# Seven block products for eight in the output projection of six token-tile pairs

## The chip, the cores and the metric

The kernel runs on one core of one Trainium2 chip. The metric is device microseconds for one execution of the whole program. Within the core, TensorE (PE; its weight loads are PEld) multiplies into PSUM; VectorE (DVE), ScalarE (ACT) and GpSimd (POOL) work on tiles in SBUF; SyncE (SP) and ACT issue the DMAs. Each engine runs its own list of instructions strictly in order and waits at semaphores for the others.

## The reference, cut to what matters

Two groups of 1024 tokens (`g` = 0 and 1) pass through one encoder layer with shared weights. All of it is float32.

```python
h    = layer_norm(x, in_ln_g, in_ln_b)
proj = h @ w_in                        # q, k, v, gates, conv inputs, memory queries
o_da = rms_norm(softmax(q1 k1) v - lam * softmax(q2 k2) v) * silu(g_da)   # 4 heads
o_cv = b * conv3(c * h_) * silu(g_cv)
o_mx = softmax(q_m k_m) v_m * silu(g_m)                                   # 256 memory tokens
out  = concat([o_da, o_cv, o_mx]) @ w_o          # (1024 x 1024) @ (1024 x 1024)
y    = layer_norm(2 ** 0.25 * h + out, ln_g, ln_b)
```

The change concerns the last two lines. The residual `2 ** 0.25 * h` needs the mean and scale of each row of x, which are known early.

## The kernel before, in words

Every float32 product is made as three passes: each operand is split into a rounded part `hi` (float32r) and a remainder `lo`, and `hi*hi + hi*lo + lo*hi` is summed in PSUM. A pass over one 128x128 block and 512 columns is one MATMUL.

A recorder (`Flow`) sets the order. Python code runs through the PE work in order, counts it in nominal nanoseconds (`fl.pe(650)` for a step of three passes), and `after(ns, fn)` puts the instructions of other engines into their lists when that count has moved on by `ns`. These numbers only fix positions in the lists; on the chip each engine goes on as soon as its operands and buffers are there.

The body is 20 jobs: for each group, four heads and one memory job (`h` is None), each for two halves of the queries. A job has four scores (`score`: PE into two PSUM tiles `ps` of the pool `psS`, DVE takes row maxima `mx`, ACT exponentials `e`). The job before it is finished meanwhile: `turn` transposes its `e` into a `psS` tile `pt` that must have been released by ACT, ACT and DVE split `pt` into `th` and `tl`, and `av` multiplies them by v. `job_steps` puts these into slots, 20 a job; between slots `run` puts steps of the list `Fillers`, the projections, spread evenly. So `turn` comes one slot (one twentieth of the job's fillers) behind `score`.

The output projection stands at the end of the same list of fillers. `Out(g, t)` handles one tile of 128 tokens: `load` fetches the mixed heads (`mraw`) and the rows of x (`xr`); `prepare` splits `mraw` into `mixh` (ACT) and `mixl` (DVE, L160); `residual` scales x (ACT L913, DVE L914, POOL L917); `passes` makes 24 MATMULs for each half of the 1024 columns into a bank `pout` (L925), adds (L928), takes statistics (L931), and `finish` normalises with four SCALAR_TENSOR_TENSOR (L946, L949) and issues two output DMAs on ACT's queue (L954). Between L946 and L949 POOL raises the variance to -1/2 (L941, L942). `w_o` is loaded and split by `load_wo` in the last job and at the start of the projection; the first four tiles overlap the last job's `turn` and `av`. Tiles 4 to 15 stand alone.

```python
for ti, (a, b) in enumerate(((self.mh, wh), (self.mh, wl), (self.ml, wh))):
    T.matmul(self.ps, a[:, kb, :], b, start=kb == 0 and ti == 0, stop=kb == KB - 1 and ti == 2)
...
V.tensor_tensor(self.xt[:, c], self.ps, self.xt[:, c], op=ALU.add)
V.bn_stats(self.bs[:, n, :], self.xt[:, c])
```

## Time and profile before

| | us |
|---|---|
| median of three runs (1226.39 to 1227.21) | 1227.06 |
| the profiled execution, its own time | 1227.65 |
| its span, first to last instruction | 1225.8 |
| PE busy in the span (5881 MATMULs) | 1182.9 (96%) |
| DVE, ACT, POOL busy | 802.6, 425.9, 414.9 |

The profiled execution's time is 1.85 us over its span (launch and end), and 0.6 us over the median. The shares of busy time are means over stages that differ: in most of the body PE is busy almost without a break, and the other engines have room. A row of the trace gives the start, the duration, the engine, the line, the operation and output<-inputs; brackets tell how long the engine was idle before it and what released it.

### The profile page before, as it was taken

The page shows a single profiled execution, that of the slowest core. Times are in us where ns is not written, and L with a number is a line of the kernel's source. Part 1 is how long each engine was busy: PE and PEld are TensorE (multiplying, and loading weights), DVE is VectorE, ACT ScalarE, POOL GpSimd, SP SyncE. Part 2 cuts the span into 40 slices and gives each one's busy share as a digit, 9 for nine tenths or more (in the row PEclk, how much of TensorE's full clock was granted, in tenths as well). Part 3 has the DMA queues.
Part 4 walks back from the last instruction along what each step waited for, and adds up shares of the span by engine and source line. Part 5 has one row for each costly group of instructions (what it writes and reads, how often), then busy time and mean ns, then how long its engine had stood idle before and what let it go on. Part 6 is the DMA issues. An engine that isn't in the chain of part 4 may idle for free.

```text
span 1225.8 us, 15660 instructions
## 1 busy us (share of the span) xinstructions
PE 1182.9 (96%) x5881; PEld 922.5 (75%) x5881; DVE 802.6 (65%) x1156; ACT 425.9 (35%) x703; POOL 414.9 (34%) x466
## 2 busy tenths in 40 slices
PE   7899999999999999999999999999999999899997
PEld 5677777767776777778677777777777877688886
DVE  4779857665677585533667666556565456887776
ACT  4624343333332333334443323434334335212220
POOL 4754413352244340232311113023011345444443
PEclk9999999999999999999999999999999999999999
DMA  8366336433644289653312212222223359354341
GB/s 309 111 233 214 143 129 206 153 145 107 214 155 155 96 277 332 238 200 133 135 43 86 86 44 95 67 97 95 73 75 112 103 207 310 106 194 152 129 148 52
DMA packets 83644, 182.62 MB, mean 149 GB/s; under 512 B 7712, under 2 KB 26352, under 8 KB 83440
## 3 DMA queue, kind: packets, MB, share of 16 engines
q1 hardware_dynamic: 80112, 175.33, 41.0%
q10 hardware_dynamic: 3456, 6.29, 1.3%
q8 instruction: 46, 0.75, 0.2%
q14 instruction: 30, 0.25, 0.1%
HBM read 119.69 MB, written 61.91 MB: 148 GB/s over the span
## 4 chain that ended last, share of the span: by engine, by line
PE 72%; DVE 13%; ACT 4%; POOL 3%; issue 3%; DMA 3%; SPq 1%; POOLq 0%; DVEq 0%; ACTq 0%
PE pout L925 13%; PE ps L678 6%; PE pt L736 5%; DVE mx L685 3%; ACT e L686 3%; PE po L764 2%; PE pG L435 2%; PE pG L437 2%; PE pG L436 2%; PE pQ L435 2%; PE pQ L437 2%; PE pQ L436 2%; PE pV L435 2%; PE pV L436 2%; PE pV L437 2%
## 5 line engine op out<-in xcount | busy, mean ns | idle before, releaser
L686 ACT ACTIVATE e<-ps,mx 128x1024 f32<-128x1024 f32 x128 | 142.8, 1116 | 302.2 <-DVE mx L685 301.9
L685 DVE TENSOR_REDUCE mx<-ps 128x1 f32<-128x1024 f32 x128 | 150.6, 1217 | 91.4 <-PE ps L678 91.4
L925 PE MATMUL pout<-woh,mixl 128*128 128x512 f32 x256 | 100.4, 392 | 1.2 <-DVE mixl L160 1.1
L925 PE MATMUL pout<-woh,mixh 128*128 128x512 f32 x256 | 100.5, 393 | 0.0
L925 PE MATMUL pout<-wol,mixh 128*128 128x512 f32 x256 | 100.2, 391 | 0.0
L160 DVE TENSOR_TENSOR tl<-pt,th 128x1024 fp32r<-128x1024 f32 x80 | 97.2, 1216 | 3.9 <-ACT th L742 3.5
L694 DVE SCALAR_TENSOR_TENSOR e<-e,ssum,e 128x1024 f32<-128x1024 f32 x64 | 87.5, 1368 | 0.0
L742 ACT ACTIVATE th<-pt 128x1024 fp32r<-128x1024 f32 x80 | 82.1, 1026 | 12.6 <-PE pt L736 11.8
L736 PE MATMUL pt<-ident,e 128*128 128x128 f32 x512 | 67.6, 275 | 12.3 <-ACT e L686 12.3
L917 POOL TENSOR_TENSOR xr<-xr,lnrow 128x512 f32<-128x512 f32 x32 | 55.2, 1741 | 68.8 <-DVE xr L914 68.8
L736 PEld LDWEIGHTS pt<-ident,e 128*128 128x128 f32 x512 | 58.0, 141 | 26.9 <-ACT e L686 21.2
L476 POOL TENSOR_TENSOR sw<-sw,ropet 128x512 f32<-128x512 f32 x32 | 41.7, 1304 | 88.4 <-DVE sw L470 88.4
L722 POOL TENSOR_SCALAR em<-em,rm 128x256 f32<-128x256 f32 x64 | 33.4, 536 | 93.0 <-DVE rm L720 46.6
L678 PE MATMUL ps<-kh,qh 64*128 64x512 f32 x256 | 61.5, 445 | 3.2 <-DVE tl L160 2.7
L160 DVE TENSOR_TENSOR wl<-wraw,wh 128x1024 fp32r<-128x1024 f32 (+1 forms) x33 | 43.7, 1323 | 23.6 <-POOL wh L157 13.8
L925 PEld LDWEIGHTS pout<-woh,mixl 128*128 128x128 f32 x256 | 48.3, 189 | 12.4 <-DVE mixl L160 2.3
L764 PE MATMUL po<-th,vh 128*128 128x512 f32 x128 | 57.2, 447 | 0.0
L906 ACT ACTIVATE mixh<-mraw 128x1024 fp32r<-128x1024 f32 x16 | 17.0, 1060 | 115.1 <-PE pout L925 97.7
L925 PEld LDWEIGHTS pout<-wol,mixh 128*128 128x128 f32 x256 | 48.4, 189 | 10.2
L925 PEld LDWEIGHTS pout<-woh,mixh 128*128 128x128 f32 x256 | 48.3, 189 | 9.9
L678 PE MATMUL ps<-kl,qh 64*128 64x512 f32 x256 | 53.5, 391 | 1.8 <-DVE kl L479 1.8
L678 PE MATMUL ps<-kh,ql 64*128 64x512 f32 x256 | 53.2, 390 | 0.0
(284 smaller groups left out, 3069.3 us busy)
## 6 DMA issues: line engine op xcount, KB each, us to landing
wp<-w SPq DMA_DIRECT2D x80, 512.0 KB, 4.3
wraw<-in_wt SPq DMA_DIRECT2D x32, 512.0 KB, 4.5
w<-wh SPq DMA_DIRECT2D x28, 512.0 KB, 5.5
w<-wl SPq DMA_DIRECT2D x28, 512.0 KB, 3.9
mraw<-mix SPq DMA_DIRECT2D x16, 512.0 KB
xr<-in_x SPq DMA_DIRECT2D x16, 512.0 KB, 6.4
out<-xr ACTq DMA_DIRECT2D x24, 256.0 KB, 2.0
x<-in_x SPq DMA_DIRECT2D x8, 512.0 KB, 5.5
```

What stands on the lines that cost most here:

```text
L160: (eng or V).tensor_tensor(out, x, hi.bitcast(F32), op=ALU.subtract)
L435: T.matmul(ps, wh[:, k], hh, start=kb == 0, stop=False)
L436: T.matmul(ps, wh[:, k], hl, start=False, stop=False)
L437: T.matmul(ps, wl[:, k], hh, start=False, stop=kb == KB - 1)
L678: T.matmul(ps[c][:, n], q[r, qt * P:(qt + 1) * P], k[r, n], start=i == 0, stop=i == 2)
L685: V.tensor_reduce(mx[:, c:c + 1], ps[c], AX.X, ALU.max, negate=True)
L686: A.activation(e[c], ps[c], AF.Exp, bias=mx[:, c:c + 1], accum_out=sm[:, c:c + 1])
L694: V.scalar_tensor_tensor(e[0], e[1], st, e[0], op0=ALU.mult, op1=ALU.add)
L736: T.transpose(pt[:, u * HS + i * P:u * HS + (i + 1) * P], self.tiles[i][:, (b + u) * P:(b + u + 1) * P], const["ident"])
L742: A.activation(th, pt, AF.Copy)
L764: T.matmul(self.po, vh[:, k, :], th[:, c], start=k == 0, stop=False)
L925: T.matmul(self.ps, a[:, kb, :], b, start=kb == 0 and ti == 0, stop=kb == KB - 1 and ti == 2)
```

## The change

Tiles 0 to 3 of group 0 go on as before (their `Out` gets its residual ready-made). The other 12 tiles go in six `Pair`s of two neighbouring tiles. A pair is one 2x2 block product: the rows are its two tiles, the inner dimension and the columns are cut in two. It is made in Winograd's form, with 7 products of 4 k-blocks each (12 MATMULs a product, 84 a pair; before, two tiles took 96). Four sums of the left operand (S1 to S4) are made on POOL for each pair (`sums`), and split on ACT and DVE (`splits`). The four sums of blocks of `w_o` (T) are made once. The products land in four PSUM regions (`pa`, `pb`, `pcd`), and `after_product` combines them into the two residual tiles `x1`, `x2` on DVE and POOL.

What can be made early is parked in DRAM in jobs 11 to 17: `park_wo` (16 blocks of `w_o` split, and 16 sums of blocks split) and `park_residual` (16 tiles of x made into the residual, through two buffers `wraw`). `load_wo`, `load_sums`, `load_rows` and `residuals` fetch these at the end. All pairs but the last normalise their second tile by another way (`mixed`): POOL makes -mean*scale, ACT applies it to 1024 columns, DVE multiplies by `ln_g`, POOL adds `ln_b`.

`job_steps` has 28 slots instead of 20, with `turn` two slots behind `score`; scores of memory jobs come two at a time. The third pair of weight buffers (`deep`) is used up to job 9 only, since `wraw` is needed for parking.

```diff
-            out.append([lambda s=s: job.score(s)])
+            if not job.mem:
+                out.append([lambda s=s: job.score(s)])
+            else:
+                out.append([lambda i=i: job.score(i) for i in (s, s + 1)] if s % 2 == 0 else [])
...
-            out.append([lambda s=s: prev.turn(s)] if prev else [])
-            out += [[], []]
+            out += [[], [lambda s=s: prev.turn(s)] if prev else [], [], [], []]
...
+    def park_unit(n, x, dst):
+        hi = sb([P, HS], F32R, ("kmh", "kml")[n % 2], "whi")
+        hi_of(hi, x)
+        after(1500, lambda: V.tensor_tensor(x, x, hi.bitcast(F32), op=ALU.subtract))
...
+    def park_residual(i):
...
+        x = sb([P, D], F32, "wraw", "xres")
+        dma(x, X[g][t * P:(t + 1) * P, :])
+        st = stats[g]
+        after(4000, lambda: A.activation(x, x, AF.Identity, bias=st[:, 0, t:t + 1], scale=st[:, 1, t:t + 1]))
+        after(5500, lambda: V.tensor_tensor(x, x, resid["g"], op=ALU.mult))
+        for n in range(2):
+            c = slice(n * HS, n * HS + HS)
+            after(7000, lambda n=n, c=c: G.tensor_tensor(x[:, c], x[:, c], resid["b"][n], op=ALU.add))
+        after(10500, lambda: dma(r_d[g][t * P:(t + 1) * P, :], x))
...
-            raw = sb([P, HS], F32, "ev", "woraw")
-            dma(raw, wo[kb * P:(kb + 1) * P, n * HS:(n + 1) * HS])
...
+            for t, src in zip(W[kb, n], wo_d[kb, n]):
+                dma(t.bitcast(F32), src)
...
+        def close(n, c):
+            G.tensor_tensor(y[:, c], y[:, c], W["lb"][n], op=ALU.add)
+            after(2000, lambda: out(c))
...
+        nb = sb([P, 1], F32, "small", "nbo")
+        G.tensor_tensor(nb, mv[:, 0:1], ve, op=ALU.mult)
+        G.tensor_scalar(nb, nb, -1.0, 1.0, op0=ALU.mult, op1=ALU.mult)
+        after(1500, lambda: A.activation(y, y, AF.Identity, bias=nb, scale=ve))
+        for n, c in enumerate(halves):
+            after(2800 + FD * n, lambda n=n, c=c: V.tensor_tensor(y[:, c], y[:, c], W["lg"][n], op=ALU.mult))
+            after(4000 + 1700 * n, lambda n=n, c=c: close(n, c))
...
+        ORDER = (("A", 0, 0, None), ("S12", 1, 1, 1), ("A", 1, 0, None), ("S12", 0, 2, 0), ("S34", 0, 3, 2), ("S34", 1, 2, None),
+                 ("A22", 0, 3, 3))
...
+            G.tensor_tensor(s1, m2[:, lo], m2[:, hi], op=ALU.add)
+            G.tensor_tensor(s2, s1, m1[:, lo], op=ALU.subtract)
+
+            def rest():
+                G.tensor_tensor(s3, m1[:, lo], m2[:, lo], op=ALU.subtract)
+                G.tensor_tensor(s4, m1[:, hi], s2, op=ALU.subtract)
+            self.rest = after(4000, rest)
...
+            if i == 0:
+                self.s1 = sb([P, HS], F32, "ev", "s1")
+                A.activation(self.s1, f[0], AF.Copy)
+            if i == 1:
+                self.u = sb([P, HS], F32, "ev", "u")
+                V.tensor_tensor(self.u, f[1], self.s1, op=ALU.add)
+                G.tensor_tensor(x1[:, hi], x1[:, hi], self.u, op=ALU.add)
+                G.tensor_tensor(x2[:, lo], x2[:, lo], self.u, op=ALU.add)
+            if i == 2:
+                V.tensor_tensor(x1[:, lo], f[0], x1[:, lo], op=ALU.add)
+                stat_of(x1, 0, self.bs[0])
+                if nxt:
+                    nxt.sums()
+                    nxt.splits("A")
+            if i == 3:
+                self.s5 = sb([P, HS], F32, "ev", "s5")
+                A.activation(self.s5, f[2], AF.Copy)
+                G.tensor_tensor(x2[:, hi], x2[:, hi], self.s5, op=ALU.add)
+                if nxt:
+                    nxt.splits("S12")
+            if i == 4:
+                w = sb([P, HS], F32, "ev", "w7")
+                V.tensor_tensor(w, f[3], self.u, op=ALU.add)
+                V.tensor_tensor(x2[:, hi], x2[:, hi], w, op=ALU.add)
+            if i == 5:
+                V.tensor_tensor(x1[:, hi], f[2], x1[:, hi], op=ALU.add)
+                stat_of(x1, 1, self.bs[0])
+                normalise(self.g, 2 * self.p, x1, self.bs[0][0], False)
+            if i == 6:
+                V.tensor_tensor(x2[:, lo], f[3], x2[:, lo], op=ALU.add)
+                stat_of(x2, 0, self.bs[1])
+                stat_of(x2, 1, self.bs[1])
+                normalise(self.g, 2 * self.p + 1, x2, self.bs[1][0], nxt is not None)
+                if nxt:
+                    nxt.splits("S34")
+                    nxt.splits("A22")
```

The order of DVE at the boundary of two tiles before: a tile's residual multiply and split stand between the two column halves of the tile before it, and only the two last operations wait for POOL (`veo`).

```order
L914 TENSOR_TENSOR xr<-xr,lnrow_9155 128x1024
L160 TENSOR_TENSOR mixl<-mraw,mixh 128x1024
L928 TENSOR_TENSOR xr<-pout,xr 128x512
L931 BN_STATS bso<-xr 128x6
L939 BN_AGGR mvo<-bso 128x2
L946 SCALAR_TENSOR_TENSOR xr<-xr,mvo,lnrow_9221 128x512 x2
L949 SCALAR_TENSOR_TENSOR xr<-xr,veo,lnrow_9223 128x512 x2
```

The order of DVE now, from the last statistics of one pair, through the first three products of the next, into its last ones (`al`, `sh` and `a2l` are remainders of a pair's operands, made while the pair before it is multiplied; L1033 is the multiply of the mixed normalisation):

```order
L1000 BN_AGGR mvo<-bso 128x2
L161 TENSOR_TENSOR sh<-sums,sh 128x512 x2
L161 TENSOR_TENSOR a2l<-mraw,a2h 128x512
L1033 TENSOR_TENSOR xr<-xr,lg 128x512 x2
L1147 TENSOR_TENSOR u<-pb,s_10550 128x512
L1151 TENSOR_TENSOR xr<-pa,xr 128x512
L996 BN_STATS bso<-xr 128x6
L161 TENSOR_TENSOR al<-mraw,ah 128x1024
L161 TENSOR_TENSOR sh<-sums,sh 128x512 x2
L1164 TENSOR_TENSOR w_10642<-pcd,u 128x512
L1165 TENSOR_TENSOR xr<-xr,w_10642 128x512
L1167 TENSOR_TENSOR xr<-pcd,xr 128x512
```

The multiply L1033, which needs POOL's `nbo` and then ACT, has come to stand ahead of `u` and of every split that follows.

The order of POOL in one tile before:

```order
L917 TENSOR_TENSOR xr<-xr,lnrow_9157 128x512 x2
L941 TENSOR_SCALAR veo<-mvo 128x1
L942 TENSOR_TENSOR veo<-veo,mhalf 128x1
```

The order of POOL now, in the same stretch as DVE's (two more pairs of `veo` follow; the sums are those of the next pair):

```order
L1029 TENSOR_TENSOR nbo<-mvo,veo 128x1
L1030 TENSOR_SCALAR nbo<-nbo 128x1
L1021 TENSOR_TENSOR xr<-xr,lb 128x512
L1148 TENSOR_TENSOR xr<-xr,u 128x512
L1149 TENSOR_TENSOR xr<-xr,u 128x512
L1021 TENSOR_TENSOR xr<-xr,lb 128x512
L1091 TENSOR_TENSOR sums<-mraw 128x512
L1092 TENSOR_TENSOR sums<-sums,mraw 128x512
L1159 TENSOR_TENSOR xr<-xr,s_10619 128x512
L1095 TENSOR_TENSOR sums<-mraw 128x512
L1096 TENSOR_TENSOR sums<-mraw,sums 128x512
```

A pair has nine operations of 512 columns on POOL, where two tiles had four, and the sums of the next pair stand behind the finish of the pair before.

The order of PE at a `turn` before, in the first job of group 1's heads:

```order
L766 MATMUL po<-tl,vh 128x512
L435 MATMUL pQ<-hTh_1_4604,wp 128x512
L436 MATMUL pQ<-hTl_1_4605,wp 128x512
L437 MATMUL pQ<-hTh_1_4604,wp 128x512
L736 MATMUL pt<-ident,e_5452 128x128
```

The order of PE at the same place now:

```order
L777 MATMUL po<-tl,vh 128x512
L446 MATMUL pQ<-hTh_1_4608,wp 128x512
L447 MATMUL pQ<-hTl_1_4609,wp 128x512
L448 MATMUL pQ<-hTh_1_4608,wp 128x512
L446 MATMUL pQ<-hTh_1_4610,wp 128x512
L447 MATMUL pQ<-hTl_1_4611,wp 128x512
L448 MATMUL pQ<-hTh_1_4610,wp 128x512
L747 MATMUL pt<-ident,e_5456 128x128
```

One filler step of three MATMULs has moved from behind the transposes to ahead of them; so it is in nearly every head job.

## Rows read from the trace of the kernel before

**Rows 1.** Windows: from:to, us; each engine busy (count); PEclk; DMA share; GB/s.
```profile
600.00:818.00 218.00, 212.37 (x1086) 160.60 (x1086) 140.41 (x207) 84.67 (x132) 35.80 (x40) 1.00 0.23 80
818.00:932.00 114.00, 113.47 (x584) 88.45 (x582) 66.79 (x101) 40.27 (x63) 21.97 (x29) 1.00 0.25 87
...
1080.00:1218.00 138.00, 137.82 (x608) 113.64 (x606) 102.95 (x141) 24.19 (x22) 63.09 (x50) 1.00 0.38 135
...
1048.00:1054.00 6.00, 5.51 (x21) 4.50 (x22) 5.90 (x8) 1.29 (x2) 2.92 (x4) 0.72 0.51 172
```

**Rows 2.** Timeline of DVE over one tile of the output projection: start, us, what.
```profile
1141.70 0.69 DVE L928 TENSOR_TENSOR xr<-pout,xr 128x512 f32<-128x512 f32 x1 [0.83 <-PE pout L925]
1142.42 0.69 DVE L931 BATCH_NORM_STATS2 bso<-xr 128x6 f32<-128x512 f32 x1
1143.15 0.21 DVE L939 BATCH_NORM_AGGREGATE mvo<-bso 128x2 f32<-128x12 f32 x1
1143.40 1.42 DVE L946 SCALAR_TENSOR_TENSOR xr<-xr,mvo,lnrow 128x512 f32<-128x512 f32 x2
1145.25 1.41 DVE L949 SCALAR_TENSOR_TENSOR xr<-xr,veo,lnrow 128x512 f32<-128x512 f32 x2 [0.44 <-POOL veo L942]
...
1150.53 1.22 DVE L160 TENSOR_TENSOR mixl<-mraw,mixh 128x1024 fp32r<-128x1024 f32 x1
1152.58 0.69 DVE L928 TENSOR_TENSOR xr<-pout,xr 128x512 f32<-128x512 f32 x1 [0.83 <-PE pout L925]
```

**Rows 3.** Timeline of POOL in the same tile.
```profile
1143.45 0.75 POOL L941 TENSOR_SCALAR veo<-mvo 128x1 f32<-128x1 f32 x1 [0.18 <-DVE mvo L939]
1144.28 0.94 POOL L942 TENSOR_TENSOR veo<-veo,mhalf 128x1 f32<-128x1 f32 x1
1150.69 3.46 POOL L917 TENSOR_TENSOR xr<-xr,lnrow 128x512 f32<-128x512 f32 x2 [5.47 <-DVE xr L914]
```

**Rows 4.** Timeline of ACT and its DMA queue in the same tile.
```profile
1146.04 1.00 ACTq L954 DMA_DIRECT2D out<-xr  x2
...
1148.12 1.23 ACT L913 ACTIVATE xr<-xr,st 128x1024 f32<-128x1024 f32 x1
```

**Rows 5.** Timeline of the program's end: the last MATMUL and the last normalisation.
```profile
1217.43 0.39 PE L925 MATMUL pout<-woh,mixl 128*128 128x512 f32 x1
...
1221.41 1.41 DVE L949 SCALAR_TENSOR_TENSOR xr<-xr,veo,lnrow 128x512 f32<-128x512 f32 x2 [0.44 <-POOL veo L942]
```

**Rows 6.** Lines of the kernel: count, duration ns min/median/max, first and last start.
```profile
L917 POOL TENSOR_TENSOR xr<-xr,lnrow x32: 1285/1726/2211, 1033.3 to 1207.3; 128x512 f32<-128x512 f32 x32
...
L306 DVE TENSOR_TENSOR xt<-xt,hhi x16: 685/692/1778, 177.7 to 458.0; 128x512 f32<-128x512 f32 x16
...
L237 POOL TENSOR_TENSOR st<-nm,st x16: 189/190/1266, 21.4 to 153.4; 128x1 f32<-128x1 f32 x16
```

**Rows 7.** As before, one ACT split of 512 columns.
```profile
L478 ACT ACTIVATE kh<-rt x16: 617/622/644, 74.5 to 855.9; 128x512 fp32r<-128x512 f32 x16
```

**Rows 8.** Waits of PE, 600 to 1000 us: total us, times, longest.
```profile
PE pt L736 <- ACT e L686: 4.8, 14, 0.7
```

**Rows 9.** The same, 100 to 600 us.
```profile
PE pt L736 <- ACT e L686: 9.7, 7, 2.2
```

**Rows 10.** The same, 1000 to 1226 us.
```profile
PE po L760 <- DVE tl L160: 3.8, 4, 2.4
```

**Rows 11.** Timeline of PE at one turn.
```profile
659.41 0.39 PE L435 MATMUL pCC<-hTh,wp 128*128 128x512 f32 x1
...
660.52 1.09 PE L736 MATMUL pt<-ident,e 128*128 128x128 f32 x8 [0.25 <-ACT e L686]
```

**Rows 12.** The page's DMA issues: count, KB each, median us to landing.
```profile
wp<-w SPq DMA_DIRECT2D x80, 512.0 KB, 4.3
...
w<-wl SPq DMA_DIRECT2D x28, 512.0 KB, 3.9
```

More of the change, by code (lines that the diff above doesn't have):

```diff
@@ L211, in encoder @@
     st_d = dt_([2, S], "stat")
+    wo_d = dt_([KB, 2, 2, P, HS], "wo")
+    wt_d = dt_([4, 4, 2, P, HS], "wot")
+    r_d = [dt_([S, D], f"res{g}") for g in range(2)]
     h_d = [dt_([KB, 2, P, HS], f"h{i}") for i in range(2)]
@@ L386, in __init__ @@
             self.i = self.k = self.bank = 0
-            self.tiles = [(it[0], it[1]) if it[0] not in ("do", "out") else None for it in items]
+            self.tiles = [(it[0], it[1]) if it[0] not in ("do", "out", "pair") else None for it in items]
         def done(self):
@@ L412, in step @@
             name, j, g, half = self.items[self.i]
+            if name == "pair":
+                pairs[j].step(self.k // 4, self.k % 4)
+                self.k += 1
+                if self.k == 28:
+                    self.i += 1
+                    self.k = 0
+                return True
             if name == "out":
-                outs[8 * g + j].passes(half, self.k)
+                outs[j].passes(half, self.k)
                 self.k += 1
@@ L908, in prepare @@
             self.late = after(1500, lambda: lo_of(self.ml, self.mr, self.mh))
-        def residual(self):
-            xt, st = self.xt, stats[self.g]
-            ag, ab = W["rows"][0:2]
-            A.activation(xt, xt, AF.Identity, bias=st[:, 0, self.t:self.t + 1], scale=st[:, 1, self.t:self.t + 1])
-            after(1000, lambda: V.tensor_tensor(xt, xt, ag, op=ALU.mult))
-            for n in range(2):
-                c = slice(n * HS, n * HS + HS)
-                after(2200 + 2000 * n, lambda c=c: G.tensor_tensor(xt[:, c], xt[:, c], ab[:, c], op=ALU.add))
         def passes(self, n, kb):
@@ L982, in encoder @@
         until.append(len(its))
-    outs = [Out(g, t) for g in range(2) for t in range(8)]
+    outs = [Out(0, t) for t in range(4)]
+    pairs = [Pair(0, 2), Pair(0, 3)] + [Pair(1, p) for p in range(4)]
+    for p, q in zip(pairs, pairs[1:] + [None]):
+        p.nxt = q
     def start_out():
@@ L988, in start_out, with do @@
         outs[1].load()
+        outs[0].residual()
         after(4000, outs[0].prepare)
-    def rows_out():
-        load_rows()
-        after(3000, lambda: [G.tensor_scalar(r, r, ALPHA, 1.0, op0=ALU.mult, op1=ALU.mult) for r in W["rows"][:2]])
-        after(4000, outs[0].residual)
-    def ahead(t, what, ns=0):
-        def go():
-            for w in what.split():
-                after(ns, getattr(outs[t], w)) if ns else getattr(outs[t], w)()
-        return ("do", go)
+    def do(fn, ns=0):
+        return ("do", (lambda: after(ns, fn)) if ns else fn)
@@ L1002, in encoder, with tail_done @@
+    tail = []
+    def tail_done():
+        assert tail, "the sums' buffers are not free yet"
     n_last = len(its) - 1
-    its[n_last:] = [("do", rows_out), its[n_last], ("do", load_rows), ("do", outs[1].prepare), ("do", lambda: load_wo(1, W1))]
-    its[n_last - 1:n_last - 1] = [("do", lambda: after(1500, start_out))]
+    its[n_last + 1:] = [do(outs[1].prepare), do(lambda: load_wo(1, W1)), do(lambda: load_sums(2, ("kh", "kl")))]
+    its[n_last - 1:n_last - 1] = [do(start_out, 1500)]
     until[-1] = len(its)
-    its += [ahead(2, "load"), ("out", 0, 0, 0), ahead(1, "residual"), ahead(2, "prepare", P2), ("out", 1, 0, 0), ahead(2, "residual"),
-            ahead(3, "load"), ("out", 2, 0, 0), ("out", 0, 0, 1), ahead(3, "prepare residual"), ahead(4, "load"),
-            ("out", 1, 0, 1), ("out", 2, 0, 1)]
@@ L1009, in encoder @@
-    for t in range(3, 16):
-        its += [("out", t % 8, t // 8, 0)]
-        if t < 15:
-            its += [ahead(t + 1, "prepare residual")]
-        if t < 14:
-            its += [ahead(t + 2, "load")]
-        its += [("out", t % 8, t // 8, 1)]
+    its += [do(outs[2].load), ("out", 0, 0, 0), do(outs[2].prepare, P2), do(outs[2].residual), ("out", 1, 0, 0), do(load_rows),
+            ("out", 2, 0, 0), ("out", 0, 0, 1), do(outs[3].load), ("out", 1, 0, 1), do(outs[3].prepare), do(pairs[0].load),
+            ("out", 2, 0, 1), do(tail_done), ("out", 3, 0, 0), do(lambda: load_sums(1, ("e0", "e0"))), do(lambda: load_sums(0, ("e0", "e0"))),
+            do(pairs[0].sums), do(lambda: pairs[0].splits("A"), 3000), do(lambda: pairs[0].splits("S12"), 4500),
+            do(lambda: pairs[0].splits("S34"), 6000), do(lambda: pairs[0].splits("A22"), 7000),
+            ("out", 3, 0, 1), do(lambda: load_sums(3, ("vh", "vl")))]
@@ L1016, in encoder @@
+    its += [("pair", i, 0, 0) for i in range(len(pairs))]
     fillers = Fillers(its)
@@ L1065, in encoder @@
             fetch_rows(n - 7, 2500)
+        if n == 11:
+            for r in range(4):
+                after(6000 + 38000 * r, lambda r=r: park_wo(r))
+            for i in range(16):
+                after(RP + 6000 * i, lambda i=i: park_residual(i))
         if 2 <= n <= 6:
```

210 lines of the change are left out of this document (162 added, 48 removed).

## The prediction

> **What bounds the kernel now.** I read the windows first. PE is busy 212.37 of 218 us and 113.47 of 114 us in the later jobs, and 137.82 of 138 us in the output projection [rows 1]: PE sets the time everywhere, so whatever removes matmuls or waits of PE counts, and other engines matter only when PE comes to wait for them. Then the tile period, from one L928 to the next: 1152.58 - 1141.70 = 10.88 us for 48 matmuls, 0.2267 us each [rows 2]. DVE fills 102.95 and POOL 63.09 of the 138 us there [rows 1], with slack, but far from idle.
>
> Third, the end: the last matmul starts at 1217.43 and ends at 1217.82 [rows 5]. Twelve tiles of 10.88 us end there, so tiles 4 to 15 begin at 1087.2; from there to the end of the span (1225.8) are 138.6 us. That is the stretch which the pairs replace. Of it, 8.0 us lie behind the last matmul, and 3.0 of these behind the last L949 (1221.41 + 1.41) [rows 5].
>
> Fourth, the waits of PE: `pt` on ACT's `e` costs 4.8 us in 14 waits from 600 to 1000 [rows 8] and 9.7 us in 7 from 100 to 600 [rows 9]; `po` on `tl` costs 3.8 us at the end [rows 10].
>
> **Pairs: what PE saves.** 84 matmuls by 0.2267 are 19.04 us a pair, against 21.76 for two tiles. Six pairs alone would take 114.2 us. Behind the last product the finish is longer: the add and two statistics (3 x 0.72 from L928 and L931) and then aggregate, two L946 and two L949 to 1146.66 (3.5 us) [rows 2], with 1.4 + 0.7 us of the same engine's work for the other tile still in front, so about 11.3 us instead of 8.0. That is 125.5 against 138.6, or -13.1 us, if PE remains the bound.
>
> **Pairs: what the other engines need.** I do not think it does. The engines are in-order, and the new lists make a loop from one pair to the next. Starting at the BN_AGGR of a pair's second tile:
> - POOL makes `veo` (0.75 + 0.94) [rows 3] and `nbo` (two operations of one column, near 0.19 [rows 6]): 2.05 us.
> - ACT applies it to 1024 columns, 1.23 [rows 4]: 3.3.
> - DVE's first L1033, 0.69: 4.0. `u` and all splits that come later stand behind it on DVE.
> - POOL does `close`, two adds of `u`, `close`, then the sums s1 and s2 of the next pair: 6 x 1.29, the least of L917 [rows 6]: 11.7.
> - ACT splits s2, 0.63 [rows 7]: 12.35; DVE takes the remainder `sh`, 0.69: 13.05.
> - DVE: `w`, the add to x2, the add to x1, its statistics, 4 x 0.72: 15.9; aggregate and two L946, 1.66: 17.6; two L949, 1.45: 19.0; the add to x2 and two statistics: 21.2 [rows 2]. Then the next BN_AGGR.
>
> So even undisturbed the loop takes 21.2 us, more than PE's 19.04: DVE, POOL and ACT are each idle for part of it, but one after the other. In the tile loop before nothing like it exists: only L949 waits for POOL, 0.44 us [rows 2].
>
> What is disturbed is the open price. POOL's L917 takes 1285 ns at least, 1726 in the median and 2211 at most, and DVE's L306 once 1778 instead of 692 [rows 6]. In the tile read here two L917 take 3.46 us, from 1150.69 on [rows 3], beside an L160 that runs until 1151.75 [rows 2]; 2 x 1.29 from there on ends at 1154.3, 0.15 beyond the 1154.15 measured. So a POOL add does not progress while a two-operand DVE operation runs, and the converse. The Trainium skill's page "SBUF — State Buffer", section "🔬 SBUF: two separate sides", calls this an exclusive lock on a shared pair of ports, held for a whole instruction; this trace agrees (2211 ns is 1285 plus most of an L160's 1.22 us). By the page alone any DVE operation with two SBUF inputs counts, the adds out of PSUM not.
>
> Along the loop I count these collisions: `veo`/`nbo` behind the three remainders that DVE does just then (+0.7); `close` behind the second L1033 (+0.6); POOL's six adds with the 1.22 us `al` in between (+0.95); `sh` and the adds to x2 against the sums (+0.8); `veo` behind L946 (+0.44, the gap in [rows 2]). Sum 3.5, so a period L of 24.7 us. The bounds are 0 (L 21.2) and, if every one of nine POOL adds had the median 1726 instead of 1285, +4.0 (L 25.2).
>
> From the pairs' start to the first pair's BN_AGGR: 7 products, of which the sixth ends at 16.3, x1's finish until 20.9, x2's 2.2: 23.1, with collisions 24.7. Four more periods (the fifth pair's BN_AGGR), then the last pair, whose multiplies still stand behind a mixed finish: 5.4 to the end of L1033, five POOL adds to 11.5, two adds and one statistic to 13.6, aggregate to L949 3.55, x2's add and statistics 2.15, its finish 3.55, and 3.0: 25.9. That is 24.7 + 4 x 24.7 + 25.9 = 149.4 us against 138.6: +10.8. With L = 21.2, and 24.8 for the last: 23.2 + 84.8 + 24.8 = 132.8, -5.8. The break-even with the 138.6 is near L = 22.2. PE then waits some 5 us a pair for operands that stand behind POOL's sums.
>
> To this I add 1.5 us for the first `mraw` of pair 1, which stand on SP behind twelve loads of 512 KB for the sums of `w_o` (6 MB; at the 172 GB/s which 0.51 of the DMA engines' time gave [rows 1], full use would take 18 us, of which most lies under the tile before and the first three products, 10.9 and 8.2 us). Bounds 0 and 4.5. Pair stage: +12.
>
> **`turn` one slot later.** One filler step of three matmuls, 0.68 us, has moved ahead of most `turn`s. In the turn shown, the filler ends at 659.8 and the transposes wait 0.25 us for `e` [rows 11]. The 14 waits of at most 0.7 go wholly: -4.8 [rows 8]. The 7 earlier ones lose 0.7 each: -4.9 [rows 9]. Against it, the next `score` has one step less ahead of it, and its `ps` is released later; I give back 2. Sum -7.7; bounds -14.5 (all waits go) and 0 (all given back).
>
> **Parking.** From 600 to 818 DVE gets 32 remainders and 12 sums at 0.69: 30.4 on top of 140.41 of 218. From 818 to 932 it gets 16 multiplies of 1.22: 19.5 on top of 66.79 of 114; POOL gets 32 adds of 1.29 (41.3 on 21.97), ACT 16 of 1.23 (19.7 on 40.27) [rows 1, 2, 4, 6]. All of it fits beside PE, but each instruction can stand in front of a `tl` or `mx` for which PE waits. Of 50 us inserted on DVE I let about a tenth reach PE: +4.5. Bounds 0 (PE's slack hides it) and 14 (over a quarter).
>
> **Start of the projection.** Loading `w_o` no longer splits it on DVE and POOL. The 3.8 us of waits for `tl` [rows 10], and 1.7 us for the low clock in 1048 to 1054 (6 us at 0.72 [rows 1]), can go: -5.5. In exchange some 9 MB must arrive between 1029 and 1057; at 172 GB/s with the DMA engines half busy [rows 1] that is 27 us at full use, with no room, and up to 5 us of waits. I take -4; bounds -5.5 and +5.
>
> **Sum.** +12 - 7.7 + 4.5 - 4 = +4.8 us on the profiled 1227.65: 1232.4. That execution is 0.6 above the median, so the forecast is 1232.
>
> **Rivals.**
> - *PE stays the bound* (faster). If collisions cost little, or the loop overlaps better than I walked it, L is at most 22.2: with -13.1 to 0 for the pairs, 1207 to 1219, centre 1214. For it: DVE and POOL have idle time in each period, and L949 loses only 0.44 to POOL before. Against it: the loop is of dependencies, not of load, and takes 21.2 without a collision.
> - *In between*: L 22.2 to 23.5, 1220 to 1227.
> - *The residual's two buffers* (slower). Load 4.3 [rows 12], ACT 1.23, DVE 1.22, two POOL adds 2.58 and a store of 3.9 [rows 12] are 13.2 us for a buffer, and with two buffers one is needed every 12 us of the recorder's count, about 13 us real. If it takes a microsecond more, the loads on SP are late by that much 7 times each, and the weights queue behind them: +7 us, on top of my sum, 1239 or over. It decides from a cycle of 13 us on. Against it: DMA is busy only 0.25 there [rows 1].
>
> **How the numbers follow.** Forecast (L 23.5 to 25.5, 1227 to 1239) 0.48; PE-bound 0.30; in between 0.10; two buffers 0.12. What a measurement here can tell from no change is 0.2%, or 2.5 us: 1224.6 to 1229.5. Faster: 0.30 and 0.06 of the in-between. Same: 0.02 of it and 0.12 of the forecast. Slower: the forecast's other 0.36, 0.12, and 0.02. Range: 1212, which leaves out the PE-bound case's lower part (0.12), to 1243 (0.06 above it); the forecast's own range is 1227 to 1239.
>
> **What would show it.** From the first pair on, PE should have gaps in every pair, at `pb` or `pcd`, released by DVE, and a period near 24.7 us between BN_AGGRs of second tiles; DVE should wait before L1033 for ACT, and POOL's L1148, L1021 and L1091 should have medians over 1.29. The `pt` waits between 600 and 1000 should be near 0. The forecast is wrong if the period is near 19 to 21 and PE is busy through the stage, or if the loss or gain lies before 1029.

## The result and the profile after

The changed kernel takes 1278.37 us (median of 4 runs, 1277.11 to 1280.18) against 1226.72 for the kernel before, a ratio of 1.0426 with a 95% interval of 1.041 to 1.0441. It is 52 us slower; the forecast was 5. The profiled execution has a span of 1275.3 us against 1225.8, so 49.5 us are to be found in the trace.

Up to tile 4, or pair 0, both programs issue the same 5305 MATMULs (5113 of the body, 192 of the first four tiles) nearly in one order, so the start of the n-th one can be compared:

| start of MATMUL number | before, us | after, us | difference |
|---|---|---|---|
| 2800 | 584.2 | 577.2 | -7.0 |
| 3800 (parking of w_o lies ahead) | 787.0 | 788.6 | +1.6 |
| 4600 (parking of the residual lies ahead) | 944.1 | 962.2 | +18.0 |
| 5112 (in the projection's first tiles) | 1039.8 | 1055.0 | +15.2 |
| start of tile 4, or of pair 0 | 1087.0 | 1098.5 | +11.5 |
| end of the span | 1225.8 | 1275.3 | +49.5 |

So three stretches cost time, and two win some. Windows of the profile after (from:to, length; busy time and count of PE, its weight loads, DVE, ACT, POOL; granted clock, DMA share, GB/s):

```profile
640.00:800.00 160.00, 150.90 (x762) 116.33 (x763) 126.06 (x181) 56.77 (x87) 52.51 (x64) 0.99 0.56 194
800.00:960.00 160.00, 146.65 (x731) 112.29 (x730) 113.21 (x139) 71.00 (x98) 86.49 (x73) 0.99 0.61 209
1098.00:1266.00 168.00, 129.50 (x507) 96.52 (x505) 105.14 (x145) 33.66 (x49) 94.11 (x82) 0.96 0.38 133
```

PE, nearly without a break in [rows 1] (idle for 5.6 us of 218, 0.5 of 114 and 0.2 of 138), is now idle for 9.1, 13.4 and 38.5 us. No other engine is full in its place: DVE reaches 126 of 160. The waits of PE from 600 to 1000 (total, times, longest):

```profile
PE ps L689 <- DVE tl L161: 13.8, 12, 2.5
PE pt L747 <- ACT e L697: 10.0, 7, 2.6
```

and from 1080 to the end:

```profile
PE pcd L1134 <- ACT s L1158: 11.9, 6, 7.1
PE pcd L1134 <- DVE w L1164: 11.5, 6, 2.4
PE pa L1134 <- ACT s L1144: 8.5, 5, 1.7
PE pcd L1134 <- DVE xr L1167: 4.7, 6, 0.8
```

The first pair of lines answers to [rows 8]: where `pt` waited 4.8 us, `pt` and `ps` together wait 23.8 (`ps` waited 1.2 before). From 100 to 600 the `pt` waits are 5.1 us in 6 places, against [rows 9]; the 3.8 us for `po` in [rows 10] are 0.8.

In the pair stage the second tiles' BN_AGGRs start at 1135.34, 1161.70, 1189.56, 1215.90, 1243.81 and 1268.63. The walk was for the first 24.7 us behind the start of the stage; it came after 36.9. Then four periods of 26.3 to 27.9, against 24.7. From the fifth to the end 31.5, against 25.9. Two places show why. One is a middle pair's DVE timeline (start, duration, what; brackets: idle before, and releaser):

```profile
1149.50 1.52 DVE L161 TENSOR_TENSOR sh<-sums,sh 128x512 fp32r<-128x512 f32 x1 [0.15 <-ACT sh L1114]
1150.94 0.68 DVE L1164 TENSOR_TENSOR w<-pcd,u 128x512 f32<-128x512 f32 x1
1151.71 0.99 DVE L1165 TENSOR_TENSOR xr<-xr,w 128x512 f32<-128x512 f32 x1
1154.77 0.69 DVE L1167 TENSOR_TENSOR xr<-pcd,xr 128x512 f32<-128x512 f32 x1 [2.07 <-PE pcd L1134]
```

with PE's at the same time, only the rows that waited:

```profile
1146.25 3.04 PE L1134 MATMUL pcd<-wot,sh 128*128 128x512 f32 x12 [0.96 <-ACT s L1158]
1151.68 0.50 PE L1134 MATMUL pcd<-woh,sh 128*128 128x512 f32 x1 [2.38 <-DVE w L1164]
1155.52 0.73 PE L1134 MATMUL pcd<-wot,a2h 128*128 128x512 f32 x2 [0.78 <-DVE xr L1167]
```

The product that begins at 1151.68 adds to the first half of `pcd`. It waits for `w`, which reads the second half. The two halves are one tile of the pool, and the wait is for the tile. The two other rows are of the same kind: the fifth product, into the second half, waits for the copy `s` of the first, and the seventh, into the second, for the add that reads the first. DVE then waits 2.07 us for the sixth product, in the middle of the loop.

The other place is the first pair. SP's issues (a duration over some 0.3 us each is waiting):

```profile
1086.64 9.10 SPq L473 DMA_DIRECT2D out<-xr  x4
1095.79 0.43 SPq L967 DMA_DIRECT2D wot<-wot  x1
...
1095.79 9.83 SPq L967 DMA_DIRECT2D wot<-wot  x12
1106.39 5.89 SPq L978 DMA_DIRECT2D mraw<-mix  x2
```

Four stores of the first tiles' outputs hold the twelve loads of sums back until 1095.8. Pair 1's `mraw` comes behind them, and ACT and POOL, in order, stand at it with pair 1's splits in front of pair 0's copies:

```profile
1117.58 1.06 ACT L1114 ACTIVATE ah<-mraw 128x1024 fp32r<-128x1024 f32 x1 [15.44 <-DMA mraw<-mix]
1118.55 0.58 ACT L1158 ACTIVATE s<-pcd 128x512 f32<-128x512 f32 x1
```

Behind that gap PE (7.14 us of it idle, up to 1119.18) also has the low clock. Windows:

```profile
1114.00:1117.00 3.00, 0.00 (x0) 0.00 (x0) 0.00 (x0) 0.00 (x0) 0.00 (x0) 0.92 1.18 305
1117.00:1120.00 3.00, 0.82 (x2) 0.73 (x3) 1.23 (x1) 1.54 (x2) 0.71 (x1) 0.50 1.02 308
1120.00:1123.00 3.00, 3.00 (x8) 2.32 (x8) 1.21 (x1) 1.19 (x2) 2.92 (x3) 0.50 0.57 218
```

At 0.50, the 1.2 GHz level, 8 MATMULs run in the last 3 us; at 0.2267 us each it would be 13. The walk left this out.

### The profile page after: what moved, and what is told of

Same layout as the page of the kernel before. It is cut to its first block, busy times and chain, and to the rows that moved or that the text cites. A ratio compares the mean times of both kernels' runs of the same rounds, so it can differ in the third digit from the quotient of the medians.

```text
span 1275.3 us, 16065 instructions
## 1 busy us (share of the span) xinstructions
PE 1181.1 (93%) x5809; PEld 912.8 (72%) x5809; DVE 854.6 (67%) x1210; ACT 450.2 (35%) x744; POOL 508.4 (40%) x549
## 5 line engine op out<-in xcount | busy, mean ns | idle before, releaser
L689 PE MATMUL ps<-kh,qh 64*128 64x512 f32 x256 | 70.2, 444 | 16.9 <-DVE tl L161 16.9
L747 PE MATMUL pt<-ident,e 128*128 128x128 f32 x512 | 67.8, 276 | 14.7 <-ACT e L697 14.7
L951 POOL TENSOR_TENSOR xres<-xres,ab 128x512 f32<-128x512 f32 x32 | 50.1, 1586 | 40.4 <-DVE xres L948 18.8
L689 PEld LDWEIGHTS ps<-kh,qh 64*128 64x128 f32 x256 | 30.8, 183 | 48.1 <-issue 25.1
L689 PE MATMUL ps<-kl,qh 64*128 64x512 f32 x256 | 60.7, 398 | 1.8 <-DVE kl L490 1.8
L161 DVE TENSOR_TENSOR wl<-wraw,wh 128x1024 fp32r<-128x1024 f32 (+1 forms) x33 | 43.0, 1304 | 23.8 <-POOL wh L158 13.8
L158 POOL TENSOR_SCALAR wh<-wraw 128x1024 fp32r<-128x1024 f32 (+1 forms) x32 | 32.9, 1030 | 53.3 <-PE pG L447 12.3
L777 PE MATMUL po<-tl,vh 128*128 128x512 f32 x128 | 51.1, 399 | 0.0
L776 PE MATMUL po<-th,vl 128*128 128x512 f32 x128 | 50.9, 397 | 0.0
L305 POOL TENSOR_TENSOR xt<-xt,shift 128x512 f32<-128x512 f32 x16 | 23.8, 1486 | 63.8 <-DVE xt L302 22.1
L1134 PE MATMUL pcd<-wot,sh 128*128 128x512 f32 x144 | 37.8, 413 | 11.9 <-ACT s L1158 11.9
L488 POOL TENSOR_TENSOR rt<-rt,sw 128x512 f32<-128x512 f32 x32 | 46.5, 1452 | 2.5
```

The costliest lines, as they stand in the source:

```text
L161: (eng or V).tensor_tensor(out, x, hi.bitcast(F32), op=ALU.subtract)
L689: T.matmul(ps[c][:, n], q[r, qt * P:(qt + 1) * P], k[r, n], start=i == 0, stop=i == 2)
L747: T.transpose(pt[:, u * HS + i * P:u * HS + (i + 1) * P], self.tiles[i][:, (b + u) * P:(b + u + 1) * P], const["ident"])
L776: T.matmul(self.po, vl[:, k, :], th[:, c], start=False, stop=False)
L777: T.matmul(self.po, vh[:, k, :], tl[:, c], start=False, stop=end)
L951: after(7000, lambda n=n, c=c: G.tensor_tensor(x[:, c], x[:, c], resid["b"][n], op=ALU.add))
```

## Experiments

The kernels are the changed one with the edit shown, unless something else is said; times are medians against about 1226 us for the kernel before.

**The new slots alone.** On the kernel before:

```diff
-            out.append([lambda s=s: prev.turn(s)] if prev else [])
-            out += [[], []]
+            out += [[], [lambda s=s: prev.turn(s)] if prev else [], [], [], []]
```

(with the paired scores of memory jobs). Expected: 

> The kernel before with the new slots of `job_steps` alone: `turn` two of 28 slots behind `score` in place of one of 20, the scores of memory jobs two at a time. Theory (the 7 to 8 us that the changed kernel is ahead at matmul 3000 come from it): and it wins the 4.8 us of the later jobs too: 1215 to 1220. Rival (what was won in the early jobs is the low clock at 393, and the next score's `ps` waits take the rest back): 1223 to 1227.

Measured 1216.40 us, ratio 0.9918 (0.9903 to 0.9933): 10.4 us won. PE's waits from 600 to 1000 in this kernel are

```profile
PE ps L678 <- DVE tl L160: 2.2, 3, 1.0
PE pt L736 <- ACT em L715: 1.0, 1, 1.0
```

and none of 14 waits for `e` is left. Two low clocks are gone as well: in the kernel before, the granted clock is 0.83 from 270 to 280 and from 390 to 400, here it is 1.00 in both. By MATMUL 4600 the lead is 15.3 us (7.5 at MATMUL 2000 and 7.8 at 2800, with the first memory job in between, so the pairing of scores is not what gave it); 3.3 are given back at the start of the projection, where `po` waits 6.9 us for `tl`. The theory holds.

**No parking of w_o.**

```diff
-                after(6000 + 38000 * r, lambda r=r: park_wo(r))
...
-            for t, src in zip(W[kb, n], wo_d[kb, n]):
+            for t, src in zip(W[kb, n], h_d[n][kb]):
```

Expected: 

> The changed kernel without `park_wo`: the last stage fetches blocks of the same size from the scratch of h in place of the split and summed w_o, so w_o is left out. Theory (its 44 DVE and 36 POOL operations delay `tl` and `mx`, 9 to 10 us by matmul 3000 to 3800): 1267 to 1270. Rival (the loss of that stretch is the new order of score and turn, with one filler step less ahead of a score): under 3 us won, 1275 or more, and PE still waits for `tl` at `ps`.

Measured 1263.67 us: 14.7 us won, more than the 9 to 10 expected. At MATMUL 3800 this kernel leads the one before by 13.1 us, just as the new slots alone do (13.3); the changed kernel's +1.6 hid that lead. So the parking costs 15 us there.

**The same parking without DVE.**

```diff
-        after(1500, lambda: V.tensor_tensor(x, x, hi.bitcast(F32), op=ALU.subtract))
...
+            block(t2, r, 0)
...
-                V.tensor_tensor(b22, b22, b12, op=ALU.subtract)
...
-                V.tensor_tensor(t2, b22, b11, op=ALU.add)
-                V.tensor_tensor(b21, b21, t2, op=ALU.subtract)
```

Expected: 

> The changed kernel with `park_wo` in place, but without its 44 DVE operations (the remainders are not taken and three of four sums are not made, one buffer is filled by a load instead; w_o is lost); POOL's operations and all loads and stores stay. Theory (DVE's operations, each 0.69 us and some standing at POOL's result, delay `tl` and `mx`): most of the 14.7 us that the kernel without `park_wo` won: 1264 to 1268. Rival (SP, in order, stands for the stores at POOL's results, and the weights come late; or the DMA traffic): under 5 us won, 1273 or more.

Measured 1263.31 us, 15.1 won: as much as without the parking. In its windows

```profile
640.00:790.00 150.00, 150.00 (x784) 116.28 (x783) 96.10 (x142) 57.27 (x88) 49.16 (x64) 1.00 0.64 222
```

PE is busy throughout, with POOL's work (49.16 us) and 222 GB/s of traffic still there. In the changed kernel the same stretch reads

```profile
640.00:790.00 150.00, 140.90 (x710) 108.64 (x711) 117.07 (x167) 52.75 (x81) 51.27 (x62) 0.99 0.55 192
```

With 21 us more of DVE's work, at 78% busy, PE loses 9.1 us of the 150. The price of this parking is shown to be DVE's instructions, with what they wait for, and not POOL's own, nor the DMA's.

**No parking of the residual.**

```diff
-                after(RP + 6000 * i, lambda i=i: park_residual(i))
...
-            dma(x, r_d[g][(2 * p + j) * P:(2 * p + j + 1) * P, :])
+            dma(x, X[g][(2 * p + j) * P:(2 * p + j + 1) * P, :])
```

Expected: 

> The changed kernel without `park_residual`: the pairs load rows of x in place of the parked residual (as many bytes), so what is left out is the scaling of x. Theory (the parked residual costs 16 us where it is made, by matmul 3800 to 4600): 1261 to 1264. Rival (the loss there is left from the parking of w_o, whose stores and late weights go on, or the waits come back elsewhere): under 6 us won, 1272 or more.

Measured 1259.63 us: 18.7 won. From 800 to 940 PE is busy 140.00 of 140 us.

**The residual's parking, cut in four ways**: without the store, without DVE's multiply, without ACT's scaling, without both.

```diff
-        after(10500, lambda: dma(r_d[g][t * P:(t + 1) * P, :], x))
```
```diff
-        after(5500, lambda: V.tensor_tensor(x, x, resid["g"], op=ALU.mult))
```
```diff
-        after(4000, lambda: A.activation(x, x, AF.Identity, bias=st[:, 0, t:t + 1], scale=st[:, 1, t:t + 1]))
```

Expected without the store: 

> The changed kernel with `park_residual` in place, but its result not stored (the 16 stores are left out, and the pairs load rows of x in place of it, so the scaling of x is lost); all 64 operations of ACT, DVE and POOL stay. Theory (two buffers: a load waits until the store of the last but one has landed, comes late, and ACT, in order, stands 18.8 us at the scaling, in front of the exponentials): with the store gone the loads are in time, ACT's waits go, 12 to 18 us are won, 1260 to 1266. Rival (the inserted operations themselves delay `tl` and `e`): under 6 us won, 1272 or more.

Measured 1276.93 us, 1.4 won. ACT's waits for loads from 820 to 940, 17.6 us in 8 places, are gone, and PE's waits there fall only from 13.4 to 8.3; the granted clock in 860 to 900 is 0.91 against 0.96. My theory here, that the rotation of two buffers is the price, falls.

Expected without the multiplies: 

> The changed kernel with `park_residual` in place but without its 16 multiplies on DVE (the scaling by a row of x's norm is left out); ACT's, POOL's and SP's part stays. Theory (as with w_o, each DVE instruction put between the others delays `tl` and `mx`, and PE has no slack there: 19.5 us of multiplies and 12 us of waiting for ACT): 12 to 18 us won, 1260 to 1266. Rival (ACT's scalings in front of the exponentials, and the wait of 18.8 us for loads): under 5 us won, 1273 or more.

Measured 1269.82 us (1269.01 to 1276.78), 8.5 won: between theory and rival. In the profiled execution, the longest of the four, ACT stands at the loads for 28.8 us from 780 to 960.

Expected without the scalings: 

> The changed kernel with `park_residual` in place but without ACT's 16 scalings (the norm of x is left out); DVE's multiplies wait for the loads themselves. Theory (DVE's work is the price): under 6 us won, 1272 or more; it may even lose, since DVE, in order, now stands at the late loads. Rival (ACT standing at the loads is the price): 12 us or more won, 1266 or less.

Measured 1271.16 us (1268.24 to 1273.99), 7.2 won, again between. DVE stands at the loads for 9.4 us.

Expected without both: 

> The changed kernel with `park_residual` in place but without DVE's multiplies and without ACT's scalings (POOL's adds, the loads and the stores stay, and POOL waits for the loads itself). Theory (the 18.7 us of this parking are what is put into the lists of both engines on the way from a score to the next, 8.5 us for DVE's part alone and 7.2 us for ACT's alone): both together 14 to 18 us won, 1260 to 1265. Rival (leaving one out only lets the other stand at the late loads; what costs is the late loads, by POOL too, or the traffic): under 10 us won, 1268 or more.

Measured 1265.34 us (1262.91 to 1267.27), 13.0 won, a little under the theory's 14 to 18. The delay gained from MATMUL 3800 to 4600 is 4.0 us in place of 16.4. So most of this parking's price is what DVE and ACT do between a score and the next. The parts add up roughly (8.5 + 7.2 = 15.7 against 13.0). Of the 5.7 us that remain, the profile shows the larger part. From 800 to 940 PE waits once, and the wait goes back to a late load:

```profile
904.46 1.09 PE L747 MATMUL pt<-ident,e 128*128 128x128 f32 x8 [2.74 <-ACT e L697]
900.27 1.76 DVE L161 TENSOR_TENSOR kl<-qms,kh 128x512 fp32r<-128x512 f32 x1 [5.93 <-POOL kh L158]
898.36 1.29 POOL L833 TENSOR_TENSOR og<-og,rb 128x512 f32<-128x512 f32 x1 [9.88 <-DMA rb<-rd]
```

`e` waits for `mx`, which stands behind `kl`; `kl` waits for `kh`, which stands on POOL behind `og`. The load of `rb` is issued at 893.64, right behind a load of `xres` at which SP, in order, had stood for 7.6 us until an earlier store of `xres` had landed. So the two buffers do cost something, here 2.7 us and the low clock behind it (0.91 from 900 to 920); no run removes this alone.

One place of the changed kernel shows how it happens, on DVE:

```profile
848.70 1.23 DVE L948 TENSOR_TENSOR xres<-xres,ag 128x1024 f32<-128x1024 f32 x1 [3.80 <-ACT xres L947]
...
850.35 2.02 DVE L705 SCALAR_TENSOR_TENSOR e<-e,ssum,e 128x1024 f32<-128x1024 f32 x1
852.30 1.75 DVE L490 SCALAR_TENSOR_TENSOR kl<-rt,kh 128x512 fp32r<-128x512 f32 x1
853.97 1.21 DVE L161 TENSOR_TENSOR tl<-pt,th 128x1024 fp32r<-128x1024 f32 x1
...
856.33 2.03 DVE L948 TENSOR_TENSOR xres<-xres,ag 128x1024 f32<-128x1024 f32 x1
858.28 2.34 DVE L696 TENSOR_REDUCE mx<-ps 128x1 f32<-128x1024 f32 x2
```

on POOL:

```profile
850.01 3.49 POOL L951 TENSOR_TENSOR xres<-xres,ab 128x512 f32<-128x512 f32 x2 [3.65 <-DVE r L702]
```

and on PE:

```profile
855.24 0.50 PE L689 MATMUL ps<-kh,qh 64*128 64x512 f32 x1 [2.35 <-DVE tl L161]
...
860.79 1.09 PE L747 MATMUL pt<-ident,e 128*128 128x128 f32 x8 [0.20 <-ACT e L697]
```

DVE first stands 3.80 us at a parked multiply, which waits for ACT's parked scaling, itself held up 1.23 us by its load. Two operations behind it run beside POOL's parked adds and take 2.02 and 1.75 us, where their medians in this program are 1.29 and 0.69. So `tl` ends at 855.18, and PE, whose score needs the bank that `tl` releases, has waited 2.35 us. Then the next multiply, here 2.03 us, stands in front of `mx`; `mx` releases `e`, and `e` the transposes, which wait 0.20 us; these release `tl`, and `tl` the next score's bank. Each score begins where the last one left, so a delay is carried on instead of being absorbed in the idle time that DVE has elsewhere.

**Two PSUM tiles.**

```diff
-                    s = psS.tile([P, S], F32, tag="s", name="pcd")
-                    self.f += [s[:, 0:HS], s[:, HS:S]]
+                    self.f += [psS.tile([P, S], F32, tag="s", name=nm)[:, 0:HS] for nm in ("pc", "pd")]
```

Expected: 

> The changed kernel with the products of `pcd` in two PSUM tiles, one for each half, instead of two halves of one tile; nothing else moves. Theory (the wait is for the tile, not for the data): the sixth product waits for `w`, which reads the other half, 2.4 us in each pair, and DVE then waits 2.07 us for it at L1167, on the loop from pair to pair; with two tiles both waits go, the period of the BN_AGGRs falls from 26.4 to 27.9 us to about 24.3, and with the low clock behind the long gaps the time falls by 12 to 16 us, to 1262 to 1266. Rival (the loop is set by POOL and DVE excluding each other, and PE only follows): DVE's wait at L1167 moves to another place, under 3 us are won, 1275 to 1278.

Measured 1263.95 us, 14.4 won, and the periods are 24.1 to 24.2. The theory holds, and its 24.3 with it. The loop now reads as it was walked. From the BN_AGGR at 1157.07 to the next at 1181.15, POOL's six adds begin behind L1033 and run without a gap until 1170.36, and ACT's split and DVE's remainder follow at once:

```profile
1161.47 1.66 POOL L1021 TENSOR_TENSOR xr<-xr,lb 128x512 f32<-128x512 f32 x1 [2.08 <-DVE xr L1033]
...
1168.20 2.16 POOL L1092 TENSOR_TENSOR sums<-sums,mraw 128x512 f32<-128x512 f32 x1
```
```profile
1170.40 0.64 ACT L1114 ACTIVATE sh<-sums 128x512 fp32r<-128x512 f32 x1 [0.67 <-POOL sums L1092]
```
```profile
1171.07 1.55 DVE L161 TENSOR_TENSOR sh<-sums,sh 128x512 fp32r<-128x512 f32 x1
1172.54 0.68 DVE L1163 TENSOR_TENSOR w<-pd,u 128x512 f32<-128x512 f32 x1
```

The waits of PE that are left in a middle pair are others:

```profile
1149.22 0.73 PE L1133 MATMUL pd<-wot,a2h 128*128 128x512 f32 x2 [0.81 <-DVE w L1163]
1161.20 0.50 PE L1133 MATMUL pa<-woh,ah 128*128 128x512 f32 x1 [3.39 <-ACT s L1143]
```

**DVE's normalisation for all tiles** (with two PSUM tiles):

```diff
-                normalise(self.g, 2 * self.p + 1, x2, self.bs[1][0], nxt is not None)
+                normalise(self.g, 2 * self.p + 1, x2, self.bs[1][0], False)
```

Expected: 

> The kernel with two PSUM tiles (1263.95 us, period 24.1), and every tile normalised by the four DVE operations, none by POOL, ACT, DVE and POOL in turn (L1033 and L1021 are gone). Theory (the loop from pair to pair runs through that mixed finish: ACT's 1.24 us of it stands in front of the copy of `pa` for which PE waits 3.4 us, and its two POOL adds in front of the next sums): period down by 2 to 3 us, five times, and the low clock behind the wait goes: 1247 to 1256. Rival (DVE is the bound; it gets 1.5 us more a pair): period up, 1264 to 1271.

Measured 1274.15 us: 10 us lost; the rival was right in the sign, but the cause is another, as the next run shows. ACT's timeline:

```profile
1162.65 1.00 ACTq L1011 DMA_DIRECT2D out<-xr  x2
1163.70 0.60 ACT L1143 ACTIVATE s<-pa 128x512 f32<-128x512 f32 x1 [4.82 <-DVE xr L1017]
```

The copy for which PE waits now stands behind two output issues, and these behind the last scaling. DVE itself waits 4.57 us in this period.

**The same with the pairs' stores on SP.**

```diff
-            if g == 0 and t < 4:
-                store(dst, y[:, c], 3000)
-            else:
-                A.dma_start(dst, y[:, c])
+            store(dst, y[:, c], 3000)
```

Expected: 

> The kernel with two PSUM tiles and every tile normalised by DVE alone (1274.15 us, period 25.8 to 27.1), with the pairs' output stores issued by SP in place of ACT. Theory (on ACT the two stores of a pair's second tile wait for its last scaling, L1017, and the copy of `pa` stands behind them: 1163.70 against 1160.57 in the mixed form, which PE waits for 4.57 us; without them the copy is free when product one ends, and POOL's two closing adds are gone): period 20.5 to 22, so 20 to 25 us less than 1274, 1249 to 1254. Rival (with four DVE operations a tile DVE is the bound, 18 us of work in a period and waits at ACT and POOL): period over 24, 1262 or more.

Measured 1250.87 us, as the theory said; the period is 22.2, a little over its 20.5 to 22. The normalisation and the stores were moved one after the other, so no run has the stores alone.

**Pair 1's `mraw` sooner.** The first tiles' stores go to ACT's queue, and

```diff
-            ("out", 3, 0, 1), do(lambda: load_sums(3, ("vh", "vl")))]
+            ("out", 3, 0, 1)]
...
+                if i == 1 and self is pairs[0]:
+                    load_sums(3, ("vh", "vl"))
```

Expected: 

> The changed kernel with two moves on the queues: the output stores of the first four tiles go out on ACT's queue like all others (on SP they hold the loads of the sums of w_o back for 9 us, until 1095.8), and the last four of those loads come behind the loads of pair 1's `mraw`. Theory (pair 0 lasts 33.7 us in place of 26 because its DVE and ACT lists contain the splits of pair 1, whose `mraw` lands at 1119): the loads end 5 to 12 us sooner, the 7.1 us wait of PE and the low clock behind it go: 1266 to 1270. Rival (the bytes before pair 1 are what takes the time, 400 GB/s with all DMA engines busy from 1099 to 1120, and these just move): 1275 to 1278.

Measured 1273.98 us, but with runs from 1268.47 to 1274.93, between theory and rival. In the profiled one (1268.47, the shortest of the five) the first BN_AGGR comes 29.7 us behind the stage's start instead of 36.9, so the order on SP does count there. How much it is worth in the median, 4.4 us, is less certain.

**All four moves**, and then **all four without both parkings**. Expected: 

> The whole change with every operation kept, and the four moves in the last stage together: two PSUM tiles, DVE's normalisation, the pairs' stores on SP, the first tiles' stores on ACT with the last sums of w_o loaded behind pair 1's `mraw`. Theory (pair 0 lasts 34.8 us in place of 29.4 without this last move): 5 to 8 us under 1250.87, so 1243 to 1246, and with both parkings at 33 us still slower than before by 16 to 20 us. Rival (the loads of the sums are bound by bandwidth): 1249 to 1251.

Measured 1248.02 us (1244.96 to 1250.61): 2.9 us better than without the last move, undecided between theory and rival. In its profile the first BN_AGGR comes 29.5 us behind the stage's start, against 34.8 without that move. With all four moves the change is still 1.79% slower than the kernel before (1.61 to 1.96). The period is 22.2 us, and PE still waits for `w` there:

```profile
PE pd L1135 <- DVE w L1165: 8.4, 4, 2.4
```

Expected: 

> The changed kernel with two PSUM tiles, DVE's normalisation, the pairs' stores on SP, the first tiles' stores on ACT and the last sums of w_o loaded behind pair 1's `mraw`; and without both parkings (as many bytes are fetched at the end from other scratch and from x, so w_o and the scaling of x are left out). It shows what the seven products are worth when their operands cost nothing: by the sums of the single runs, 1278.4 less 18.7 and 14.7 for the parkings, less 24 for the period and 10 for pair 0: 1205 to 1215, and against the kernel with the new slots alone (1216.4) a gain of 1 to 11 us. Rival (the pair stage cannot beat the tile loop even then, because it stands at 24 us a pair or more): over 1219.

Measured 1211.72 us. Against the 1216.40 of the new slots alone that is 4.7 us. But the pair stage itself, 1066.3 to 1210.0, lasts 143.7 us, where the same tiles took 138.6 before: its period is 22.2 us, and two tiles take 21.76. What is won lies between MATMUL 4600 and the stage's start. As arranged here, seven products for eight win nothing in their own stage even when no time is spent on making the operands from `w_o` and the residual. At MATMUL 4600 this kernel stands within 1.0 us of the one with the new slots alone, where the changed kernel is 33.3 behind: the two parkings are the whole of that difference.

## Why the prediction was wrong

The sign and the loop named as the bound of the pair stage were right; three terms were far too small. By the prediction's own steps:

- *PE's saving* of 13.1 us did not come, as forecast: PE waits in every pair. (Two small figures do not follow from their own terms, the finish of 11.3 us, which adds to 10.8, and the break-even of 22.2, which is 22.4 between the two ends given; the forecast hangs on neither.)
- *The loop*, L = 24.7. With the tile wait removed the period is 24.1, inside the 21.2 to 25.2, and POOL's second sum ends 13.3 us behind the BN_AGGR, where the walk with its collisions has 14.0. The collisions are there as counted, DVE's `al` and POOL in one pair:

```profile
1143.91 2.35 DVE L161 TENSOR_TENSOR al<-mraw,ah 128x1024 fp32r<-128x1024 f32 x1
```
```profile
1143.89 1.29 POOL L1021 TENSOR_TENSOR xr<-xr,lb 128x512 f32<-128x512 f32 x1
1145.14 2.28 POOL L1091 TENSOR_TENSOR sums<-mraw 128x512 f32<-128x512 f32 x1
```

L1021 has begun 0.02 us before `al`, which then ends 1.1 us behind the end of L1021, near the 1.2 it needs alone; L1091 begins meanwhile and ends 1.2 us behind `al`. The lock of the Trainium skill's page "SBUF — State Buffer", section "🔬 SBUF: two separate sides" (the one that starts first has the ports for its whole instruction), reads just so, and this trace agrees. In the kernel as it is, though, the period was 26.3 to 27.9. **The step that failed here** is the line "`w`, the add to x2, the add to x1, its statistics, 4 x 0.72": it lets DVE go on without PE. I took PE to wait for data only, so the sixth product was long done. It waits for `w`, because two banks were one tile, and DVE then waits for it. That, with the low clock behind the gaps, cost 14.4 us. The same step failed once more in the last pair, where no splits are left in DVE's way. It was walked at 25.9 to the end and took 31.5:

```profile
1257.87 0.69 DVE L1164 TENSOR_TENSOR w<-pcd,u 128x512 f32<-128x512 f32 x1 [5.41 <-PE pcd L1134]
```

  The walk has two adds and a statistic done 13.6 us behind the fifth BN_AGGR (1243.81); here `w` only starts 14.1 us behind it, when PE's fifth product is done.
- *Late `mraw`*, +1.5, bounds 0 to 4.5. The first BN_AGGR came 36.9 us behind the stage's start; the walk's 24.7 and this term make 26.2, so it was 10.7 us late. I counted the bytes in front of it on SP, but not the four stores ahead of them that wait for DVE until 1095.8; and I let most of the transfer lie under products which themselves had ACT's copy behind a split of the late `mraw`. The shift of four loads and four stores brought 7 us of it back in one profile, the two PSUM tiles 2 (34.7 in their profile); the rest no run assigns.
- *`turn`*, -7.7, bounds 0 to -14.5: measured alone, -10.4. The reason was right: over the whole program the waits for `e` fall from 14.5 us to 5.1, near the 9.7 taken. Those of `ps` for `tl` rise from 2.7 to 5.4, a little more than the 2 given back. What the sum left out is the low clock behind two of the waits.
- *Parking*, +4.5, bounds 0 to 14: measured 14.7 and 18.7, 33 us. **This is the largest failure**: "of 50 us inserted on DVE I let about a tenth reach PE", because "all of it fits beside PE" by the sums of busy time. The price is as much as two thirds of those 50 us, but part of it is ACT's, whose 19.7 us I had put at nothing. For w_o the runs show that it is DVE alone, 15 us for 30 inserted; for the residual DVE's and ACT's instructions together make 13.0 of 18.7, for 39 inserted.
- *Start of the projection*, -4: by MATMUL number -6.6 from 4600 to the start of the stage, though 3.3 of the slots' gain are lost there in the kernel with the slots alone. Against that kernel it is -9.8, beyond the bound of -5.5: the 6.9 us of `po`, which the new slots had made out of 3.8, are 0.8 here.

The account: -15.3 for the slots and +33.3 for the parkings up to MATMUL 4600, -6.6 to the pairs, +38.0 for the pairs, of which 12 had been forecast. Sum 49.4, the span's 49.5 but for rounding. The pairs' excess of 26 is 10.7 in the first, 9.7 in the four periods and 5.6 behind the fifth.

Of the signs named, the gaps of PE came, and so did DVE's waits for ACT before L1033 (8.3 us in 5). L1091 and L1021 had medians of 2.28 and 1.48 us, but L1148 kept its 1.29, and the `pt` waits from 600 to 1000 rose to 10.0 us instead of going to 0. One sign of being wrong came too: 18.0 of the 49.5 us were lost before 1029.

Of the rivals, the one with two buffers gave a slower kernel at the right place, but the run without the store won only 1.4 us, so its reason is not what carries the loss. PE as the bound, with L at most 22.2, did not occur in the changed kernel; with all four moves the period comes to just 22.2.
